# One 8 KB tile for every place of the weight ring, another order ahead of the experts, and small experts in pieces of 2048 and 1536 columns

## The chip, the core and the metric

The kernel runs on one core of one Trainium2 chip, as one program. The time is the device time of one execution in microseconds (us); of several executions the median is given. The engines are named as the profile names them: PE is TensorE, whose weight loads are PEld; DVE is VectorE, ACT is ScalarE, POOL is GpSimd, and SP is SyncE, which here issues almost all transfers.

## The reference

Two residual layers over 256 tokens of 1024 channels, in f32. Each layer has a token mixer (a gated linear recurrence and a differential attention side by side, merged by gates, then an output projection `w_out` of 1024 x 1024) and a channel mixer. In layer 0 the channel mixer is a dense SwiGLU; in layer 1 it is a mixture of eight experts, two of them for each token. All weights are read once, in f32. Cut to what matters here:

```python
def moe_swiglu(h, router, w1, w3, w2):          # w1, w3: 8 x 1024 x 3584, w2: 8 x 3584 x 1024
    logits = t @ router
    vals, idx = lax.top_k(logits, 2)
    comb = sum(one_hot(idx, 8) * softmax(vals)[..., None])
    for e in range(8):
        out += comb[:, e] * ((silu(t @ w1[e]) * (t @ w3[e])) @ w2[e])
```

One expert's w1 and w3 hold 29.36 MB (10^6 bytes) together and its w2 14.68 MB; the eight experts hold 352.3 MB.

## The kernel before

Everything but the experts uses matmuls in which each operand is split in two: `split()` (line 132) has ACT round a weight tile into `wh` (L146) and DVE subtract to get the rest `wl` (L148), and `three()` (L157) issues three matmuls for each tile of weights. `wh` and `wl` are two tiles of 4 KB per partition, four of each. `proj_T()` (line 311) walks over a weight matrix in blocks of 256 columns with eight slabs k of 128 rows; a block is one load of 1 MiB, split in two halves u, and every half gives one group of 128 output columns, which is evacuated when its eight slabs are summed.

The scheduler of the framework orders the instructions of each engine ahead of time, from the order of the program and its own model of durations; on the chip every engine then takes its list in that order, and so does SP with the transfers.

`moe()` (line 759) ends layer 1. While `w_out` is projected, `ev_r` adds each group of the result onto the residual `xT` (L358), squares it (L263) and multiplies it with the router (L799). Then follow, in program order, `rows_rstd()` (matmuls L273, then DVE L257 and POOL L258, which give `r`, the norm of each token), `turn(1)`, which transposes the second half of the residual (PE L753, ACT L786, into `xg`), and `to_bcast()`, which spreads a gate row over the partitions (PE L251, ACT L252, into `g2b`). From `r` a chain of small DVE instructions picks the two experts of each token (L817 to L835, with matmuls L831 to L833), `slots()` builds selection matrices (L858), and `gather()` multiplies them with `xg` (L865) to get the tokens of an expert, X. Only then does the first expert's matmul start.

The experts stand at positions p = 0 to 7. Positions 0, 2, 4 and 6 hold up to 96 tokens ("big"), positions 1, 3, 5 and 7 up to 64 ("small"). An expert is done in four units i: 1024 columns of its 3584 for i = 0 to 2 and 512 for i = 3. `up()` (line 1077) multiplies X with w1 and w3 into the PSUM banks `ups` (L1090, and L1095 for the tokens 64 to 95 of a big expert); ACT and DVE make the gated product from the banks (L1101, L1102, L1107, L1108); PE transposes it (L1117); `down()` (line 1124) multiplies it with w2 into `pds` for a big expert or into `low` for a small one (L1135, L1141), and `finish()` (line 1161) adds the result onto the tokens. The units run in the order up(n), down(n-1), transposes of n, up(n+1), and so on. Experts 0 and 1 are interleaved.

The weights of the experts pass through a ring of 16 places of 1 MiB, each 8 KB in each of 128 partitions. `plan` lists the loads in the order of their use, 42 for each expert, and `ahead()` (line 1045) issues them; a load waits until PE has done with the tile that held the place. Places 0 to 10 are single tiles (six `raw`, five `raw2`, loads at L120). Place 11 is the two halves of `xT`, and places 12 to 15 are four pairs of `wh` and `wl`; these five places are filled by two loads of 512 KB each (L1066), every one of half of the slabs. A load of `up` for i = 0 to 2 takes two slabs of 1024 columns, so every row that it reads in DRAM is 4 KB long; for i = 3 it takes four slabs of 512 columns, rows of 2 KB. A load of w2 reads 8 KB in one run for each partition, or 4 KB in each of two loads where the place is split. The last two loads of the program read w2 in rows of 2 KB.

Of the kernel before, what the change touches and what calls it, by code (L numbers as in the profile page):

```python
# [8 lines left out]
F32 = mybir.dt.float32  # L9
F32R = mybir.dt.float32r  # L10
# [24 lines left out]
CAPS = (96, 64, 96, 64, 96, 64, 96, 64)  # L35
GATHER_AT = {(0, 0): (1, 2), (2, 2): (3, 4), (4, 2): (5, 6), (6, 2): (7,)}
# [12 lines left out]
def hybrid_trunk(ctx: ExitStack, tc: tile.TileContext, x, c, ada_w, ada_b, norm_mix_g, norm_ffn_g, w_in, lb_logits,  # L49
# [113 lines left out]
    const.tile([P, 120], F32, name="gap")  # L163
# [105 lines left out]
    def rows_rstd(acc, ps):  # L269

        for t in range(NT):
            for i, sq in enumerate(acc):
                t_.matmul(ps[:, t:t + 1], lhsT=sq[:, t * P:(t + 1) * P], rhs=ones[:, 0:1], start=i == 0, stop=i == 1)  # L273
        r = small([P, NT], "r", pool=keep)
        rstd(r, ps, D, NT)
        return r
# [34 lines left out]
    def proj_T(w, c0, xh, xl, nk, evac, ncols, order=None):  # L311
# [447 lines left out]
    def moe(y, l, pdp):  # L759
# [15 lines left out]
        small([P, 8], "gap", bufs=1)  # L775
        xs = [small([P, D], "xs") for _ in range(NT)]
# [26 lines left out]
        proj_T(w_out[l], 0, y[0], y[1], KD, ev_r, D)  # L803


        r = rows_rstd(acc, lp[0][:, NE:NE + NT])
# [4 lines left out]
        turn(1)  # L811
        g2b = to_bcast(row, 2, small([P, D], "g2b", bufs=1))
# [125 lines left out]
        def dns(p):  # L938

            return pds if CAPS[p] > 64 else [low]  # L940

# [56 lines left out]
        units = [(0, 0), (0, 1), (1, 0), (0, 2), (1, 1), (0, 3), (1, 2), (1, 3)] + [(p, i) for p in range(2, NE) for i in range(4)]  # L998
        last_ = NE - 1, 3

        def half_of(i):
            return 512 if i < 3 else 256

        def up_srcs(p, i):
            n, c0 = half_of(i), i * 1024
# [5 lines left out]
        def down_srcs(p, i):  # L1011
            n = half_of(i)
            rows_ = n // P

            def view():
                return moe_w2[0, which(p)].rearrange("o (c p k) f -> p (o c) k f", p=P, k=rows_)
            if (p, i) == last_:
                for c in range(2):
                    yield lambda c=c: [view()[:, i * 1024 // n + h, :, c * 512:(c + 1) * 512] for h in range(2)]
                return  # L1020
            for k0 in range(0, rows_, 2):
                for h in range(2):
                    yield lambda c=i * 1024 // n + h, k0=k0: view()[:, c, k0:k0 + 2, :]
# [21 lines left out]
        def ahead(n):  # L1045

            while len(loaded) < min(n, len(plan)):
                src, turn_ = plan[len(loaded)](), len(loaded) % slots_
                k = 4 if isinstance(src, list) else src.shape[1]
                if turn_ >= RAW_BUFS + RAW_MORE:  # L1050
                    if turn_ == RAW_BUFS + RAW_MORE:
                        halves = [xt.rearrange("p k t -> p (k t)") for xt in xT]
                    else:
                        halves = [splp.tile([P, 1024], F32, tag=tag, name=nm("raw")) for tag in ("wh", "wl")]
                else:
                    tag = {"pool": phase[0], "tag": "raw2", "bufs": RAW_MORE} if turn_ >= RAW_BUFS else {"pool": rawp, "tag": "raw"}
                    raw = tag.pop("pool").tile([P, 2048], F32, name=nm("raw"), **tag)
                    halves = [raw[:, h * 1024:(h + 1) * 1024] for h in range(2)]
                    if not isinstance(src, list):
                        load(src, raw, k=k)  # L1060
                        loaded.append(halves)
                        continue
                if not isinstance(src, list):
                    src = [src[:, h * k // 2:(h + 1) * k // 2, :] for h in range(2)]
                for half, part in zip(halves, src):
                    nc.sync.dma_start(half.rearrange("p (k f) -> p k f", k=k // 2), part)  # L1066
# [10 lines left out]
        def up(p, i, xp):  # L1077

            n, rows_, big = half_of(i), half_of(i) // P, CAPS[p] > 64
            nk = 1024 // n  # L1080
            for k0 in range(0, KD, nk):
# [17 lines left out]
            sa = small([P, 512], "sa")  # L1099
            sv = sa[:, :n].rearrange("s (k p) -> s k p", k=rows_)  # L1100
            s_.activation(sv, in_order(ups[0][:, :n]), AF.Silu)  # L1101
            v_.tensor_tensor(sv, sv, in_order(ups[1][:, :n]), op=ALU.mult)  # L1102
            parts = [(sa, 0, P)]
            if big:
                sb = small([P, 512], "sa")
                sv = sb[64:, :n].rearrange("s (k p) -> s k p", k=rows_)
                s_.activation(sv, in_order(ups[2][:64, :n]), AF.Silu)  # L1107
                v_.tensor_tensor(sv, sv, in_order(ups[2][64:, :n]), op=ALU.mult)  # L1108
# [15 lines left out]
        def down(p, i, us):  # L1124
            rows_, dn = half_of(i) // P, dns(p)
            for k0 in range(0, rows_, 2):
                tiles = [next_tile() for _ in range(2)]
                for k in range(k0, k0 + 2):
                    first, last = i == 0 and k == 0, i == (2 if p == NE - 1 else 3) and k == rows_ - 1
# [75 lines left out]
        for n, (p, i) in enumerate(units):  # L1205
            def before_this():
                down(*before)
                if before[:2] in ((before[0], 3), (NE - 1, 2)):
# [51 lines left out]
    for l in range(DEPTH):  # L1260
# [15 lines left out]
        def end_of_mixer(then=None):  # L1276
            acc, ev_x = residual_T(lambda: ada[l, 1]["col"][:, 0:8], then)
            proj_T(w_out[l], 0, y[0], y[1], KD, ev_x, D)
# [81 lines left out]
```

## Time and profile before

| | before |
|---|---|
| median of 3 runs | 1515.84 us (1513.46 to 1518.27) |
| profiled execution, time | 1517.2 us |
| profiled execution, span of its instructions | 1515.4 us |
| mean granted TensorE clock | 0.989 |
| PE busy in the span | 1468.2 us (97%) |
| DVE, ACT busy | 629.6 us (42%), 374.0 us (25%) |
| read from memory | 503.56 MB |

The profiled execution is one execution; its time stands 1.4 us above the median. [...] Busy time of PE counts overlapped matmuls, so 97% does not mean that PE is the limit. Times in the rows are microseconds from the start of the span. The token mixers and the dense layer take the first 660 us, the experts the rest.

### The profile page before, as it was taken

How to read it: one execution, taken by the hardware profiler on the slowest of the kernel's cores; microseconds unless marked ns; L12 is line 12 of the kernel's file. 1: busy time of each engine (PE TensorE's matmuls, PEld its weight loads, DVE VectorE, ACT ScalarE, POOL GpSimd, SP SyncE). 2: the span in 40 equal slices, each digit the busy share in tenths (PEclk: the TensorE clock that was granted, in tenths of full speed). 3: DMA queues.
4: the chain of work that ended last, by engine and by line, in shares of the span. 5: the costliest groups of instructions: out<-in, count | busy, mean ns of one | idle time of the engine just before them, and what ended most of it. 6: DMA issues, size and time to landing. Idle time of an engine off the chain costs nothing.

```text
span 1515.4 us, 29680 instructions
## 1 busy us (share of the span) xinstructions
PE 1468.2 (97%) x12659; PEld 897.3 (59%) x12659; DVE 629.6 (42%) x1046; ACT 374.0 (25%) x618; POOL 33.8 (2%) x34
## 2 busy tenths in 40 slices
PE   5999999999999999999999999999999998999996
PEld 3988999999998899873333333433433433334322
DVE  4898677867788877641100211120021120111202
ACT  3534546544446545320000000000000000000000
POOL 1010100000000100000000000000000000000000
PEclk8999999999999999999999999999999999999999
DMA  9988545668796645858999999999999999999996
GB/s 369 360 300 284 189 142 171 220 225 299 267 339 227 216 146 211 293 213 324 399 418 418 417 421 419 419 420 417 415 420 411 418 420 418 418 415 417 415 423 240
DMA packets 186032, 506.62 MB, mean 334 GB/s; under 512 B 11016, under 2 KB 79252, under 8 KB 170148
## 3 DMA queue, kind: packets, MB, share of 16 engines
q1 hardware_dynamic: 185572, 504.56, 86.0%
q8 instruction: 101, 1.65, 0.4%
q14 instruction: 39, 0.32, 0.1%
q0 software_dynamic: 320, 0.09, 0.0%
HBM read 503.56 MB, written 1.05 MB: 333 GB/s over the span
## 4 chain that ended last, share of the span: by engine, by line
PE 85%; DMA 7%; issue 5%; DVE 1%; SPq 1%; ACT 1%; POOL 0%; DVEq 0%; POOLq 0%; ACTq 0%
PE mm L157 32%; PE mm L1090 24%; PE pd L1135 6%; DMA raw<-in_moe_w_dram 6%; PE at L1095 6%; PE at L1135 4%; PE pd L1141 4%; PE ms L865 2%; PE ms L532 2%; PE ms L1117 1%; DMA raw<-in_ada_w_dram 1%; PE ms L1179 1%; PE ada L229 1%; PE at L615 1%; DVE wl L148 0%
## 5 line engine op out<-in xcount | busy, mean ns | idle before, releaser
L1090 PE MATMUL mm<-raw,X 128*32 128x512 f32 (+1 forms) x3792 | 439.8, 543 | 2.2 <-DMA raw<-in_moe_w_dram 2.1
L1090 PEld LDWEIGHTS mm<-raw,X 128*32 128x32 f32 x3792 | 133.0, 110 | 223.1 <-issue 189.8
L148 DVE TENSOR_TENSOR wl<-raw,wh 128x1024 fp32r<-128x1024 f32 (+1 forms) x188 | 226.8, 1210 | 76.9 <-ACT wh L146 74.4
L146 ACT ACTIVATE wh<-raw 128x1024 fp32r<-128x1024 f32 (+1 forms) x188 | 196.6, 1048 | 177.5 <-PE mm L157 134.5
L1102 DVE TENSOR_TENSOR sa<-sa,mm 128x512 f32<-128x512 f32 (+1 forms) x32 | 19.9, 621 | 464.3 <-PE mm L1090 420.1
L1095 PE MATMUL at<-raw,X 128*32 128x512 f32 (+1 forms) x952 | 171.6, 542 | 0.0
L157 PE MATMUL mm<-hh,wh 128*128 128x256 f32 x576 | 164.2, 285 | 3.6 <-ACT wh L146 3.3
L157 PE MATMUL mm<-hl,wh 128*128 128x256 f32 x576 | 165.0, 287 | 0.0
L157 PE MATMUL mm<-hh,wl 128*128 128x256 f32 x576 | 164.9, 287 | 0.1
L1101 ACT ACTIVATE sa<-mm 128x512 f32<-128x512 f32 (+1 forms) x32 | 17.4, 544 | 516.1 <-PE mm L1090 516.1
L1135 PE MATMUL pd<-raw,u 128*32 128x512 f32 x848 | 121.5, 594 | 0.0
L157 PEld LDWEIGHTS mm<-hh,wh 128*128 128x128 f32 x576 | 110.1, 191 | 5.7 <-ACT wh L146 3.6
L157 PEld LDWEIGHTS mm<-hl,wh 128*128 128x128 f32 x576 | 109.9, 191 | 0.7 <-issue 0.7
L157 PEld LDWEIGHTS mm<-hh,wl 128*128 128x128 f32 x576 | 109.6, 191 | 0.4 <-DVE wl L148 0.4
L1135 PE MATMUL at<-raw,u 128*32 128x512 f32 x816 | 94.0, 594 | 7.0 <-DMA raw<-in_moe_w_dram 6.7
L1141 PE MATMUL pd<-raw,u 128*32 128x512 f32 x424 | 87.4, 592 | 0.0
L1095 PEld LDWEIGHTS at<-raw,X 128*32 128x32 f32 x952 | 46.4, 110 | 60.4 <-issue 54.4
L223 DVE SCALAR_TENSOR_TENSOR raw<-raw,cs,raw 128x2048 f32<-128x2048 f32 x32 | 75.1, 2347 | 8.3 <-DMA raw<-in_ada_w_dram 8.3
L157 PE MATMUL mm<-wh,hh 128*128 128x512 f32 x160 | 64.6, 404 | 0.0
L1135 PEld LDWEIGHTS at<-raw,u 128*32 128x32 f32 x816 | 25.7, 110 | 65.3 <-issue 46.3
L157 PE MATMUL mm<-wl,hh 128*128 128x512 f32 x160 | 64.0, 400 | 0.0
L1135 PEld LDWEIGHTS pd<-raw,u 128*32 128x32 f32 x848 | 31.3, 110 | 54.7 <-issue 51.2
(308 smaller groups left out, 2041.6 us busy)
## 6 DMA issues: line engine op xcount, KB each, us to landing
raw<-in_moe_w_dram SPq DMA_DIRECT2D x231, 1024.0 KB, 14.8
raw<-in_moe_w_dram SPq DMA_DIRECT2D x168, 512.0 KB, 11.1
raw<-in_ada_w_dram SPq DMA_DIRECT2D x47, 1024.0 KB, 4.9
raw<-in_w_in_dram SPq DMA_DIRECT2D x44, 1024.0 KB, 7.4
raw<-in_ffn_w_dram SPq DMA_DIRECT2D x30, 1024.0 KB, 5.1
xT<-in_moe_w_dram SPq DMA_DIRECT2D x42, 512.0 KB, 16.5
raw<-in_w_out_dram SPq DMA_DIRECT2D x8, 1024.0 KB, 4.7
raw<-in_w_branch_a_dram SPq DMA_DIRECT2D x4, 1024.0 KB, 5.1
```

The costliest lines, as they stand in the source:

```text
L146: s_.activation(wh[:, c], r[:, c], AF.Copy)
L148: v_.tensor_tensor(wl[:, c], r[:, c], wh[:, c].bitcast(F32), op=ALU.subtract)
L157: t_.matmul(ps, lhsT=lhs, rhs=rhs, start=first and i == 0, stop=last and i == 2)
L223: v_.scalar_tensor_tensor(got["acc"], raw, cs[:, k:k + 1], got["acc"], op0=ALU.mult, op1=ALU.add)
L532: t_.matmul(ps[:, at_:at_ + HD].rearrange("p (g w) -> p g w", w=H), lhsT=kq[:, h, i * P:(i + 1) * P], rhs=rhs, start=True, stop=True)
L865: t_.matmul(ps[:, i * n:(i + 1) * n], lhsT=xg[t][:, k * P:(k + 1) * P], rhs=pm[:, t, :n], start=t == 0, stop=t == NT - 1)
L1090: t_.matmul(ups[m][q:q + 32, :n], lhsT=xp[:, k, 32 * s:32 * s + 32], rhs=rhs[m][h], start=k == 0, stop=k == KD - 1)
L1095: t_.matmul(ups[2][q:q + 32, :n], lhsT=xp[:, k, 64:96], rhs=rhs[m][h], start=k == 0, stop=k == KD - 1)
L1101: s_.activation(sv, in_order(ups[0][:, :n]), AF.Silu)
L1102: v_.tensor_tensor(sv, sv, in_order(ups[1][:, :n]), op=ALU.mult)
L1135: t_.matmul(dn[0][q:q + 32, :], lhsT=us[0][:, k, 64 * h + 32 * s:64 * h + 32 * s + 32], rhs=rhs[h][c], start=first and h == 0, stop=last a ...
L1141: t_.matmul(dn[1][q:q + 32, :], lhsT=us[1][:, k, 32 * h:32 * h + 32], rhs=rhs[h][c], start=first, stop=last)
```

## The change

Four edits are made together.

1. `wh` and `wl` become the two halves of one tile of 8 KB, and the two halves of `xT` become one tile. All 16 places of the ring are then single tiles, each filled by one load of 1 MiB (only the last two loads of the program still come as pairs). The small tiles that pad the layout are moved, not resized in sum.
2. The small experts at positions 3, 5 and 7 are cut into other pieces: 2048 and 1536 columns for 3 and 5, and 2048, 1024 and 512 for 7. A load of `up` in such a wide piece takes one slab of the full width, rows of 8, 6 or 4 KB (tiles of 1 MiB, 768 KB and 512 KB). `up` uses four banks for a wide piece: `ups[0:2]`, and `ups[2]` with `low` for the second 1024 columns; the last 512 of a 1536 share one bank. The results of `down` go to `pds[0]` in place of `low`. The last piece of 512 columns keeps the old form.
3. `proj_T` gets an argument `late`, which both `w_out` projections set to 2: for the first block, both halves are split first, then slabs 0 to 5 of both groups are multiplied, and then slabs 6 and 7 of both.
4. In `moe`, `turn(1)` and `to_bcast` are held on PE behind the last matmul of `rows_rstd`.

```diff
+NARROW, WIDE = (1024, 1024, 1024, 512), (3, 5, 7)
+WIDTHS = (NARROW, NARROW, NARROW, (2048, 1536), NARROW, (2048, 1536), NARROW, (2048, 1024, 512))
...
-        wh = splp.tile([P, 1024], F32R, tag="wh", name=nm("wh"))[:, :n]
-        wl = splp.tile([P, 1024], F32R, tag="wl", name=nm("wl"))[:, :n]
+        both = splp.tile([P, 2048], F32R, tag="w", name=nm("w"))
+        wh, wl = both[:, :n], both[:, 1024:1024 + n]
...
-    xT = [const.tile([P, 4, S], F32, name=f"xT{h}") for h in range(2)]
+    const.tile([P, 96], F32, name="gap0")
+    xT_all = const.tile([P, KD, S], F32, name="xT")
+    xT = [xT_all[:, 4 * h:4 * h + 4, :] for h in range(2)]
...
+                if late and b0 == 0:
+
+                    parts = [split(raw[:, :, u * P:(u + 1) * P]) for u in range(2)]
+                    ps = [mm() for _ in range(2)]
+                    for ks in (range(kn - late), range(kn - late, kn)):
+                        for gg, (wh, wl) in enumerate(parts):
+                            for k in ks:
+                                three(ps[gg][:, :n_], xh[k // 4][:, k % 4, :], xl[k // 4][:, k % 4, :], wh[:, k, :], wl[:, k, :],
+                                      k == 0, k == nk - 1, True)
+                            if kn - 1 in ks:
+                                evac(gg, ps[gg][:, :n_])
+                    continue
...
-        proj_T(w_out[l], 0, y[0], y[1], KD, ev_r, D)
+        proj_T(w_out[l], 0, y[0], y[1], KD, ev_r, D, late=2)
...
-        r = rows_rstd(acc, lp[0][:, NE:NE + NT])
+        r = rows_rstd(acc, lp[0][:, NE:NE + NT], behind)
...
-        turn(1)
-        g2b = to_bcast(row, 2, small([P, D], "g2b", bufs=1))
+        with tc.issue_after(behind[0]):
+            turn(1)
+            g2b = to_bcast(row, 2, small([P, D], "g2b", bufs=1))
...
-            return pds if CAPS[p] > 64 else [low]
+            return pds if CAPS[p] > 64 else [pds[0] if p in WIDE else low]
...
+            if is_wide(p, i):
+                for k in range(KD):
+                    for wm in (moe_w1, moe_w3):
+                        yield lambda wm=wm, k=k: wm[0, which(p)].rearrange("o (k p) f -> p (o k) f", p=P)[:, k:k + 1, c0:c0 + WIDTHS[p][i]]
+                return
...
-                if turn_ >= RAW_BUFS + RAW_MORE:
-                    if turn_ == RAW_BUFS + RAW_MORE:
-                        halves = [xt.rearrange("p k t -> p (k t)") for xt in xT]
-                    else:
-                        halves = [splp.tile([P, 1024], F32, tag=tag, name=nm("raw")) for tag in ("wh", "wl")]
+                if turn_ > RAW_BUFS + RAW_MORE:
+                    raw = splp.tile([P, 2048], F32, tag="w", name=nm("raw"))
+                elif turn_ == RAW_BUFS + RAW_MORE:
+                    raw = xT_all.rearrange("p k t -> p (k t)")
...
+            if is_wide(p, i):
+                full = [ups[:2], [ups[2], low]][:width // 1024]
+                shared = ups[2] if width % 1024 else None
+                for k in range(KD):
+                    tiles = [next_tile() for _ in range(2)]
+                    for j, banks in enumerate(full):
+                        for m in range(2):
+                            for h in range(2):
+                                for s in range(2):
+                                    q = 32 * (2 * h + s)
+                                    t_.matmul(banks[m][q:q + 32, :], lhsT=xp[:, k, 32 * s:32 * s + 32],
+                                              rhs=tiles[m][j][:, h * 512:(h + 1) * 512], start=k == 0, stop=k == KD - 1)
```

## Rows read from the trace of the kernel before

**Rows 1.** The page's part 2: data rate in 40 slices of 37.9 us.
```profile
GB/s 369 360 300 284 189 142 171 220 225 299 267 339 227 216 146 211 293 213 324 399 418 418 417 421 419 419 420 417 415 420 411 418 420 418 418 415 417 415 423 240
```

**Rows 2.** Windows of the experts' stage: length, busy times, granted clock, DMA share, GB/s.
```profile
740.00:1490.00 750.00, 736.82 (x7078) 264.99 (x7074) 98.51 (x187) 46.32 (x84) 0.00 (x0) 1.00 1.02 418
1440.00:1460.00 20.00, 19.12 (x178) 5.99 (x174) 1.44 (x3) 1.31 (x3) 0.00 (x0) 1.00 1.02 418
1462.00:1480.00 18.00, 15.64 (x144) 4.33 (x132) 0.69 (x1) 1.19 (x2) 0.00 (x0) 1.00 1.01 426
1482.00:1492.00 10.00, 8.69 (x112) 3.20 (x102) 2.19 (x3) 0.63 (x1) 0.00 (x0) 1.00 1.04 405
1495.00:1500.00 5.00, 3.85 (x46) 1.63 (x48) 1.26 (x3) 0.77 (x2) 0.00 (x0) 1.00 0.46 174
905.00:910.00 5.00, 5.00 (x48) 1.65 (x44) 0.87 (x2) 0.60 (x1) 0.00 (x0) 1.00 1.00 419
1405.00:1420.00 15.00, 15.00 (x140) 4.59 (x136) 0.29 (x1) 0.38 (x1) 0.00 (x0) 1.00 1.02 404
1270.00:1275.00 5.00, 3.29 (x63) 1.50 (x54) 0.00 (x0) 0.39 (x1) 0.00 (x0) 1.00 1.04 425
```

**Rows 3.** The chain that ended last: start, length, what, in stretches of the experts' stage.
```profile
788.84 13.87 PE mm L1090 x128
...
1072.44 15.63 DMA raw<-in_moe_w_dram
```

**Rows 4.** Windows ahead of the first expert and at its start.
```profile
635.00:640.00 5.00, 5.00 (x25) 5.00 (x25) 2.70 (x3) 1.68 (x4) 0.00 (x0) 0.50 1.03 418
...
665.00:670.00 5.00, 4.17 (x19) 4.13 (x20) 4.25 (x26) 1.33 (x2) 0.00 (x0) 0.54 0.13 53
670.00:675.00 5.00, 5.00 (x37) 3.77 (x40) 4.22 (x20) 0.00 (x0) 0.00 (x0) 0.78 0.01 3
...
700.00:705.00 5.00, 5.00 (x43) 3.26 (x35) 0.92 (x4) 0.00 (x0) 0.00 (x0) 1.00 0.29 118
```

**Rows 5.** SP's transfers in order of time: start, length of the stretch, line, count.
```profile
662.42 0.33 SPq L1066 DMA_DIRECT2D xT<-in_moe_w_dram  x1
678.70 34.08 SPq L120 DMA_DIRECT2D raw<-in_moe_w_dram  x11
```

**Rows 6.** The page's part 6: loads of 1 MiB, count, KB, median landing.
```profile
raw<-in_moe_w_dram SPq DMA_DIRECT2D x231, 1024.0 KB, 14.8
```

**Rows 7.** PE in order of time, from the last projection to the first experts.
```profile
658.57 1.02 PE L251 MATMUL at<-sa,ident 128*128 128x512 f32 x2
...
662.54 0.36 PE L273 MATMUL ms<-ones,sqk 128*128 128x1 f32 x2
665.54 0.58 PE L831 MATMUL at<-mask,upper 128*128 128x16 f32 x2 [2.64 <-DVE wt L844]
...
667.26 6.13 PE L865 MATMUL ms<-pm,xg 128*128 128x96 f32 x32 [0.28 <-DVE pm L858]
...
702.14 3.53 PE L865 MATMUL ms<-pm,xg 128*128 128x160 f32 x24
```

**Rows 8.** ACT and DVE in order of time, at the end of the projection.
```profile
659.35 0.42 ACT L263 ACTIVATE sqk<-xT 128x256 f32<-128x256 f32 x1 [2.46 <-DVE xT L358]
...
662.95 0.16 DVE L257 TENSOR_SCALAR r<-ms 128x2 f32<-128x2 f32 x1 [3.69 <-PE ms L273]
```

**Rows 9.** PE and DVE in order of time, at the start of that projection.
```profile
624.90 0.28 PE L157 MATMUL mm<-yh,wh 128*128 128x256 f32 x1
...
629.52 0.28 PE L157 MATMUL mm<-yh,wl 128*128 128x256 f32 x1
632.87 0.39 PE L157 MATMUL mm<-yl,wh 128*128 128x256 f32 x1 [3.07 <-DVE yl L674]
...
631.79 0.69 DVE L773 TENSOR_TENSOR sa<-sa,row 128x512 f32<-128x512 f32 x1 [3.54 <-DMA sa<-in_ada_b_dram]
```

**Rows 10.** The page's part 5: matmuls of `three`.
```profile
L157 PE MATMUL mm<-hh,wh 128*128 128x256 f32 x576 | 164.2, 285 | 3.6 <-ACT wh L146 3.3
```

More of the change, by code (lines that the diff above doesn't have):

```diff
@@ L309, in norm_T, with proj_T @@
         return hs, ls
-    def proj_T(w, c0, xh, xl, nk, evac, ncols, order=None):
+    def proj_T(w, c0, xh, xl, nk, evac, ncols, order=None, late=0):
         cw, n_ = 512 if nk == 4 else 256, xh[0].shape[2]
@@ L1048, in ahead @@
                 src, turn_ = plan[len(loaded)](), len(loaded) % slots_
-                k = 4 if isinstance(src, list) else src.shape[1]
-                if turn_ >= RAW_BUFS + RAW_MORE:
-                    if turn_ == RAW_BUFS + RAW_MORE:
-                        halves = [xt.rearrange("p k t -> p (k t)") for xt in xT]
-                    else:
-                        halves = [splp.tile([P, 1024], F32, tag=tag, name=nm("raw")) for tag in ("wh", "wl")]
-                else:
[L1056 to L1066, printed above, removed]
+                if turn_ > RAW_BUFS + RAW_MORE:
+                    raw = splp.tile([P, 2048], F32, tag="w", name=nm("raw"))
+                elif turn_ == RAW_BUFS + RAW_MORE:
+                    raw = xT_all.rearrange("p k t -> p (k t)")
+                elif turn_ >= RAW_BUFS:
+                    raw = phase[0].tile([P, 2048], F32, tag="raw2", bufs=RAW_MORE, name=nm("raw"))
+                else:
+                    raw = rawp.tile([P, 2048], F32, tag="raw", name=nm("raw"))
+                halves = [raw[:, h * 1024:(h + 1) * 1024] for h in range(2)]
+                if isinstance(src, list):
+                    for half, part in zip(halves, src):
+                        nc.sync.dma_start(half.rearrange("p (k f) -> p k f", k=2), part)
+                else:
+                    load(src, raw, k=src.shape[1])
                 loaded.append(halves)
@@ L1077, in up @@
         def up(p, i, xp):
-            n, rows_, big = half_of(i), half_of(i) // P, CAPS[p] > 64
+            n, rows_, big = half_of(p, i), half_of(p, i) // P, CAPS[p] > 64
             nk = 1024 // n
-            for k0 in range(0, KD, nk):
+            width = WIDTHS[p][i]
+            full, shared = [ups[:2]], ups[2] if big else None
+            if is_wide(p, i):
[10 more added lines that the diff above has]
+                                              rhs=tiles[m][j][:, h * 512:(h + 1) * 512], start=k == 0, stop=k == KD - 1)
+                    if shared is not None:
+                        for m in range(2):
+                            for s in range(2):
+                                q = 32 * (2 * m + s)
+                                t_.matmul(shared[q:q + 32, :], lhsT=xp[:, k, 32 * s:32 * s + 32], rhs=tiles[m][1][:, :512],
+                                          start=k == 0, stop=k == KD - 1)
+            for k0 in range(0, 0 if is_wide(p, i) else KD, nk):
                 tiles = [next_tile() for _ in range(2)]
@@ L1124, in down @@
         def down(p, i, us):
-            rows_, dn = half_of(i) // P, dns(p)
+            rows_, dn = half_of(p, i) // P, dns(p)
+            end_ = len(WIDTHS[p]) - (2 if p == NE - 1 else 1)
+            if is_wide(p, i):
+                n_chunks = WIDTHS[p][i] // 512
+                chunks = [us[c // 2][:, :, 64 * (c % 2):64 * (c % 2) + 64] for c in range(n_chunks)]
+                for q0 in range(0, n_chunks, 2):
+                    for k0 in range(0, rows_, 2):
+                        for ch in range(q0, min(q0 + 2, n_chunks)):
+                            tile_ = next_tile()
+                            for k in range(k0, k0 + 2):
+                                first, last = i == 0 and ch + k == 0, i == end_ and ch == n_chunks - 1 and k == rows_ - 1
+                                for c in range(2):
+                                    for s in range(2):
+                                        q = 32 * (2 * c + s)
+                                        t_.matmul(dn[0][q:q + 32, :], lhsT=chunks[ch][:, k, 32 * s:32 * s + 32],
+                                                  rhs=tile_[k - k0][:, c * 512:(c + 1) * 512], start=first, stop=last)
+                return
             for k0 in range(0, rows_, 2):
@@ L1128, in down @@
                 for k in range(k0, k0 + 2):
-                    first, last = i == 0 and k == 0, i == (2 if p == NE - 1 else 3) and k == rows_ - 1
+                    first, last = i == 0 and k == 0, i == end_ and k == rows_ - 1
                     rhs = [[tiles[h][k - k0][:, c * 512:(c + 1) * 512] for c in range(2)] for h in range(2)]
```

57 lines of the change are left out of this document (34 added, 23 removed).

## The prediction

> **What bounds the kernel now.** I read the slices of the page first, because the four edits lie in different stages. From slice 20 on, the data rate stands between 411 and 424 GB/s until the last slice [rows 1], and over 740 to 1490 us it is 418 GB/s at a DMA share of 1.02 [rows 2]: the transfers are busy without a gap, although PE also reads as busy (736.8 of 750 us). Which of the two sets the end is read from the chain: until shortly before 1072 us it runs through PE, then it crosses to landings of weights, 15.63 us in one piece at 1072 [rows 3]. A unit of 1024 columns for a small expert takes PE 13.87 us for 8 tiles [rows 3], 1.73 us a tile, while a tile of 1.049 MB at 418 GB/s takes 2.51 us. So in the experts' stage time is bytes over rate, and PE has slack.
>
> Ahead of that stage PE decides. The 16 tiles that fit into the ring have landed by about 667 us, and the data rate falls to 53 and 3 GB/s [rows 4], because the next load waits at SP until 678.70 for PE to free the first place [rows 5]. A first expert that starts x earlier moves this and all later loads x earlier: there x counts in full.
>
> **Part 1, the transfers.** Prices by length of row in DRAM come from the tail, where the plan tells which loads are in flight. The last six tiles (6.3 MB) are read in rows of 2 KB, the eight before them (8.4 MB) in rows of 8 KB, all in whole places. Landing ends at about 1497 (174 GB/s in the window of 1495 to 1500 means 2.1 us of work), so 1482 to 1492 is 2 KB, 405 GB/s, and 1462 to 1480 is 8 KB, 426 GB/s [rows 2]. The price of 4 KB is what is left of the long window: 750 us x 418 = 313.5 MB; 1/7 of two thirds of it is 2 KB (29.9 MB, 73.7 us), 11/16 of the w2 third is 8 KB (71.8 MB, 168.6 us), and the other 211.8 MB take 507.7 us, 417 GB/s. That is 2.469, 2.397 and 2.347 us per MB for 2, 4 and 8 KB; for 6 KB, a third of the way from 8 to 4 in 1/length, 2.364.
>
> What changes its row: w2 in the five split places, 5/16 of 117.4 MB = 36.7 MB, from 4 to 8 KB; the three pieces of 2048 columns, 50.3 MB, from 4 to 8; the last 1536 of experts 3 and 5, 16.8 MB from 4 to 6 and 8.4 MB from 2 to 6. So 87.0 x 0.050 + 16.8 x 0.033 + 8.4 x 0.105 = 4.35 + 0.55 + 0.88 = 5.8 us less. Lower bound: one window of 8 KB rows shows 419 GB/s [rows 2], no better than 4 KB; then only the 0.88 remains.
>
> The 105 tiles in split places (5/16 of 336) now come as 210 loads of 512 KB; they become 105 loads. The split places fill at 404 GB/s in one stretch (1405 to 1420) and at 418 in another (1440 to 1460) [rows 2]. With all 18 rounds of 5.24 MB at 404 instead of 417 the gain would be 94 MB x 0.078 = 7.4 us, otherwise nothing; I take 1.2, near the lower end, since the mean of 417 already holds the slow stretches. Transfers together: 7.0 us less, bounds 0.9 and 13.2.
>
> [...]
>
> **Part 2, the wide units on PE.** Each matmul of 512 columns reappears with another bank; the last 512 columns need half as many matmuls, twice as wide. PE's 1.73 us a tile stays, and is hidden by the 2.51 us of the transfer. A wide piece of 2048 has four banks to read out before the next `up`: two passes of DVE, each about the 0.69 us of its pass over 128x512 [rows 9], behind the first of ACT, some 2.3 us, but the `down` of the unit before lies between (at least 2 tiles, 3.5 us of PE), so nothing is charged; uncovered, five wide pieces would cost 11.5 us. `pds[0]` is read by `finish` a whole unit before the next expert's first `down`. Tiles of 768 and 512 KB let the ring hold less in time, but a load of 1 MiB lands 14.8 us after its issue [rows 6], six times its own 2.51, so the queue stays fed. Zero.
>
> **Part 3, one tile for `wh` and `wl`, and for `xT`.** A place is now free when both halves are. The last reader is a `wh` matmul in any case, so PE waits as now: 3.6 us before 576 matmuls [rows 10]. Zero; at most one matmul of 0.285 us per wait. The first half of `xT` can no longer be loaded early: the 1 MiB goes out when `turn(1)` has read the tile, about 662.4 us as its second half does now [rows 5]. If SP has it ahead of the four loads of the places behind, these wait with it, 12.6 us of transfers, which still end before 678.70. PE needs that tile 11 tiles after its start. Zero; 2.5 us if a transfer had been waiting.
>
> **Part 4, `late`.** In layer 1 PE stands 3.07 us before a `yl` matmul, because the `yl` instructions stand on DVE behind L773, which waits 3.54 us for a small transfer [rows 9]. `late` puts 36 matmuls ahead of the last two slabs. But from 624.90 to 629.52 [rows 9], 40 starts 0.12 us apart, the list had already run 40 of the block's 48 before it stopped: the scheduler mixes the two groups already, and the new order has two fewer ahead, 0.2 us more. What DVE waits for is not touched. In layer 0 PE runs through without a gap; the second split is needed one group earlier, at most one DVE pass of 1.2 us. I take +0.2, bounds 0 and +1.4.
>
> **Part 5, the order ahead of the experts.** The last square is ready at 659.77 and the norm `r` starts on DVE at 662.95 [rows 8]. Between them PE does the two broadcasts (1.02 us each pair of records) and the transposes, and the matmuls L273 end only at 662.90 [rows 7]. The eight records of L273 cost 4 x 0.36 = 1.4 us, so without the others `r` starts at 661.2, 1.75 us earlier. The moved work is at most 662.90 - 658.57 - 1.4 = 2.9 us. It runs from 661.2 to 664.1, and L831, now ready at 665.54 - 1.75 = 663.8, is queued behind it and loses 0.3. The copies into `xg` finish before `gather` needs them. Net 1.4 us less, bounds 0 (a broadcast in front of L831 as long as the gain) and 1.75.
>
> The same move fills a hole. [...] With the moved work inside the hole I expect the clock to hold: 1.7 us less; if it falls all the same, 0.
>
> **Sum.** -7.0 + 0.2 - 1.4 - 1.7 = -9.9 us. The profiled execution took 1517.2, which gives 1507.3; it stood 1.4 above the median of 1515.84, so the median forecast is 1505.9.
>
> **The rivals.**
> *Longer rows bring little.* The rate is set by something other than the row, as the 419 at 905 to 910 would have it. Then the transfers save 0.9 and the rest 2.9: 1512. If the 426 of the end is half due to the row and half to what else the tail lacks, the rows save 2.9 in place of 5.8: 1508.8. Against both: 426 over 18 us. [...]
> *The stop before `yl` goes too.* If the new list of DVE has L773 behind the `yl` instructions, 3.07 us of waiting go, and half of at least 5 us at clock 0.50 that follow [rows 4, 9]: 5.6 more, 1500.3. Nothing in the change moves L773; only another list would.
> [...]
>
> **How the numbers follow.** Forecast, with its front and row terms within 4 us: 0.55. Little from the rows (half or none): 0.22. The `yl` stop gone: 0.12. Clock or another stop in the wide units: 0.11, of which 0.09 lie beyond the bound. About 0.3% (4.5 us, the spread of the three runs) is what can be told from no change, so faster means under 1511.3. The forecast and the `yl` case lie there, and a third of the row rival: 0.74. The rest of it, and a little of the clock case, is the same: 0.17. Slower: 0.09. The range 1499 to 1513 runs from the `yl` case to the rival without any gain from rows, and leaves 2 in 10 out.
>
> **What would show it.** Right: windows over experts 3, 5 and 7 at 421 to 426 GB/s and none near 404; L273 ahead of L251, and `r` 1.5 us after the last square, now 3.2; a clock of 1.00 during the first `gather`. Wrong: a data rate of 418 in wide pieces of 8 KB rows; SP issuing the first load into a used place of the ring still 18.9 us after the last square (now 659.77 to 678.70), where I expect 15.8; DMA share below 1.0 within the experts' stage; a clock under 1.00 in units 3, 5 or 7.

## The result and the profile after

The kernel after takes 1505.88 us (median of 6 runs, 1503.97 to 1508.63), the kernel before 1515.9 (6 runs beside them, 1513.46 to 1518.27): ratio 0.994, 95% interval 0.9925 to 0.9955. The forecast was 1505.9. The profiled execution of after took 1504.83 us with a span of 1502.9; before had 1517.2 and 1515.4.

The page's part 2 (data rate in 40 slices, here of 37.6 us) and part 6 (loads) of the kernel after answer to [rows 1, 6]:
```profile
GB/s 370 363 296 293 176 155 175 211 238 287 269 340 244 198 168 197 269 248 332 395 420 420 418 423 420 420 414 425 421 421 420 426 424 422 423 422 417 420 420 263
...
raw<-in_moe_w_dram SPq DMA_DIRECT2D x283, 1024.0 KB, 17.7
...
raw<-in_moe_w_dram SPq DMA_DIRECT2D x30, 768.0 KB, 13.9
xT<-in_moe_w_dram SPq DMA_DIRECT2D x19, 1024.0 KB, 18.3
raw<-in_moe_w_dram SPq DMA_DIRECT2D x19, 512.0 KB, 10.9
```
The slices of the experts' stage now read mostly 420 to 426, where they read mostly 415 to 420. Whole places of 1 MiB are 283 and 19 loads, the split places are gone, and a load lands 17.7 us after its issue instead of 14.8. An estimate from rate and landing time has about 7.5 MB on the way at once (421 GB/s x 17.7 us), before 6.2 (418 x 14.8), so the queue is no worse fed.

Windows of the experts' stage, kernel after (columns as in [rows 2]; the clock is the granted share of full speed):
```profile
740.00:1455.00 715.00, 711.19 (x6682) 249.13 (x6677) 99.39 (x187) 43.74 (x78) 0.00 (x0) 1.00 1.02 421
...
950.00:1060.00 110.00, 109.22 (x1042) 39.65 (x1038) 19.11 (x42) 7.17 (x13) 0.00 (x0) 1.00 1.01 420
1150.00:1270.00 120.00, 119.22 (x1136) 42.92 (x1132) 19.21 (x40) 7.77 (x14) 0.00 (x0) 1.00 1.02 424
1360.00:1455.00 95.00, 94.12 (x920) 35.07 (x916) 15.20 (x26) 6.58 (x12) 0.00 (x0) 1.00 1.02 419
...
985.00:990.00 5.00, 5.00 (x48) 1.60 (x44) 0.29 (x1) 0.38 (x1) 0.00 (x0) 1.00 0.96 390
1405.00:1420.00 15.00, 15.00 (x148) 4.53 (x144) 0.00 (x0) 0.00 (x0) 0.00 (x0) 1.00 1.01 425
1425.00:1430.00 5.00, 5.00 (x52) 1.66 (x48) 1.38 (x2) 1.10 (x2) 0.00 (x0) 1.00 1.02 388
...
1470.00:1480.00 10.00, 8.24 (x84) 2.40 (x76) 2.19 (x3) 0.63 (x1) 0.00 (x0) 1.00 1.04 407
```
The same long window of the kernel before reads:
```profile
740.00:1455.00 715.00, 705.63 (x6774) 255.35 (x6770) 96.32 (x184) 44.68 (x81) 0.00 (x0) 1.00 1.02 418
```
The window of 1405 to 1420, which stood at 404 [rows 2], stands at 425. But a window at a fixed time holds other loads in each kernel, and low ones are left: 390 at 985 to 990 with a DMA share of 0.96, 388 at 1425 to 1430, and 407 in the tail with its rows of 2 KB. The stretches around the wide pieces of experts 3, 5 and 7 (950 to 1060, 1150 to 1270, 1360 to 1455) read 420, 424 and 419; in the run without wide pieces below they read 417, 420 and 419. The predicted sign of 421 to 426 shows in one of the three. PE's idle time in the long window falls from 9.4 to 3.8 us: its slack is nearly used up. The chain of the kernel after shows the same thing from the other side (columns as in [rows 3]):
```profile
797.27 1.72 PE pd L1204 x16
799.85 1.72 PE pd L1204 x16
...
1053.17 12.15 PE pd L1192 x112
...
1263.90 17.83 DMA raw<-in_moe_w_dram
```
It crosses to the landings of weights in long pieces at 1264 us, before at 1072 [rows 3]. Until then it runs through PE: a w2 tile of a big expert takes PE 2.58 us (797.27 to 799.85), a little more than the 2.49 us of its transfer at 421 GB/s.

Ahead of the experts, kernel after: engines in order of time (columns as in [rows 5, 7, 8, 9]).
```profile
623.13 0.40 PE L159 MATMUL mm<-yh,w 128*128 128x256 f32 x2
...
631.55 0.58 PE L159 MATMUL mm<-yl,w 128*128 128x256 f32 x1 [3.52 <-DVE yl L691]
...
630.47 0.69 DVE L790 TENSOR_TENSOR sa<-sa,row 128x512 f32<-128x512 f32 x1 [3.99 <-DMA sa<-in_ada_b_dram]
...
658.71 0.42 ACT L267 ACTIVATE sqk<-xT 128x256 f32<-128x256 f32 x1 [2.43 <-DVE xT L375]
...
660.21 0.16 DVE L261 TENSOR_SCALAR r<-ms 128x2 f32<-128x2 f32 x1 [1.59 <-PE ms L277]
...
659.81 0.36 PE L277 MATMUL ms<-ones,sqk 128*128 128x1 f32 x2
660.04 1.07 PE L770 MATMUL mm<-ident,xT 128*128 128x128 f32 x8
660.94 1.88 PE L255 MATMUL at<-sa,ident 128*128 128x512 f32 x4
662.81 0.37 PE L850 MATMUL at<-mask,upper 128*128 128x16 f32 x2
...
664.12 3.81 PE L884 MATMUL ms<-pm,xg 128*128 128x96 f32 x32 [0.50 <-DVE pm L877]
667.87 1.92 PE L1141 MATMUL mm<-raw,X 128*32 128x512 f32 x16
...
674.12 5.09 SPq L122 DMA_DIRECT2D raw<-in_moe_w_dram  x4
```
Read it against [rows 7, 8]: the matmuls of the norm come first, `r` starts 1.08 us after the last square (660.21 against 658.71 + 0.42) where it was 3.18, the transposes and broadcasts run where PE was idle for 2.64 us, and the 32 matmuls of the gather take 3.81 us where they took 6.13. Against [rows 9]: the stop ahead of `yl` is still there, 3.52 us instead of 3.07, and the low clock behind it too (columns as in [rows 4]):
```profile
635.00:640.00 5.00, 5.00 (x25) 5.00 (x25) 2.29 (x3) 1.12 (x3) 0.00 (x0) 0.50 1.03 417
...
665.00:670.00 5.00, 5.00 (x47) 3.45 (x49) 4.71 (x24) 0.00 (x0) 0.00 (x0) 1.00 0.17 64
```

**Three stages.** Three landmarks of each trace divide the time: the first `yh` matmul of the last `w_out`, the end of the last square, and the first matmul of an expert. Before: 624.90, 659.77, 673.32, end 1515.4 [rows 7 to 9]. After: 623.13, 659.13, 667.87, end 1502.9. So of -12.5 us in the profiled pair, -1.8 lies ahead of `w_out`, +1.1 from there to the last square, -4.8 from there to the first expert and -7.05 in the experts. The experiments below are read by the same three lengths, since medians of different kernels lie only a few us apart.

### The profile page after: what moved, and what is told of

It reads as the page before. It is cut to its first block, busy times and chain, and to the rows that moved or that the text cites. A ratio compares the mean times of both kernels' runs of the same rounds, so it can differ in the third digit from the quotient of the medians.

```text
span 1502.9 us, 29132 instructions
## 1 busy us (share of the span) xinstructions
PE 1467.1 (98%) x12535; PEld 884.9 (59%) x12535; DVE 632.8 (42%) x1051; ACT 372.1 (25%) x613; POOL 33.8 (2%) x34
## 4 chain that ended last, share of the span: by engine, by line
PE 89%; DMA 7%; DVE 1%; SPq 1%; ACT 1%; issue 0%; POOL 0%; ACTq 0%; DVEq 0%; POOLq 0%
PE mm L159 35%; PE mm L1141 16%; PE pd L1204 7%; PE at L1146 6%; DMA raw<-in_moe_w_dram 5%; PE mm L1124 5%; PE pd L1210 4%; PE at L1124 3%; PE pd L1192 2%; PE ms L549 2%; PE at L1204 2%; PE ms L884 1%; DMA raw<-in_ada_w_dram 1%; PE ms L1170 1%; PE at L1130 1%; PE ms L1248 1%
## 5 line engine op out<-in xcount | busy, mean ns | idle before, releaser
L1141 PE MATMUL mm<-raw,X 128*32 128x512 f32 (+1 forms) x2496 | 308.4, 536 | 1.7 <-DMA raw<-in_moe_w_dram 1.7
L150 DVE TENSOR_TENSOR w<-raw,w 128x1024 fp32r<-128x1024 f32 (+1 forms) x188 | 226.8, 1210 | 75.0 <-ACT w L148 72.7
L148 ACT ACTIVATE w<-raw 128x1024 fp32r<-128x1024 f32 (+1 forms) x188 | 196.6, 1048 | 175.7 <-PE mm L159 133.2
L159 PE MATMUL mm<-hh,w 128*128 128x256 f32 x1152 | 213.0, 286 | 3.5 <-ACT w L148 3.1
L159 PEld LDWEIGHTS mm<-hh,w 128*128 128x128 f32 x1152 | 180.7, 191 | 6.1 <-ACT w L148 3.5
L159 PE MATMUL mm<-hl,w 128*128 128x256 f32 x576 | 164.9, 286 | 0.0
L1154 ACT ACTIVATE sa<-mm 128x512 f32<-128x512 f32 (+1 forms) x27 | 14.8, 550 | 512.3 <-PE mm L1141 407.7
L1204 PE MATMUL pd<-raw,u 128*32 128x512 f32 x848 | 122.0, 594 | 0.0
L159 PEld LDWEIGHTS mm<-hl,w 128*128 128x128 f32 x576 | 109.7, 190 | 0.7 <-issue 0.7
L159 PE MATMUL mm<-w,hh 128*128 128x512 f32 x320 | 104.9, 402 | 0.0
L1124 PE MATMUL mm<-raw,X 128*32 128x512 f32 x720 | 99.2, 595 | 0.0
L1210 PE MATMUL pd<-raw,u 128*32 128x512 f32 x424 | 87.7, 592 | 0.0
L1192 PE MATMUL pd<-raw,u 128*32 128x512 f32 x608 | 67.5, 593 | 1.4 <-DMA raw<-in_moe_w_dram 1.4
## 6 DMA issues: line engine op xcount, KB each, us to landing
raw<-in_moe_w_dram SPq DMA_DIRECT2D x283, 1024.0 KB, 17.7
```

What stands on the lines that cost most here:

```text
L159: t_.matmul(ps, lhsT=lhs, rhs=rhs, start=first and i == 0, stop=last and i == 2)
L1124: t_.matmul(banks[m][q:q + 32, :], lhsT=xp[:, k, 32 * s:32 * s + 32], rhs=tiles[m][j][:, h * 512:(h + 1) * 512], start=k == 0, stop=k == K ...
L1141: t_.matmul(ups[m][q:q + 32, :n], lhsT=xp[:, k, 32 * s:32 * s + 32], rhs=rhs[m][h], start=k == 0, stop=k == KD - 1)
L1192: t_.matmul(dn[0][q:q + 32, :], lhsT=chunks[ch][:, k, 32 * s:32 * s + 32], rhs=tile_[k - k0][:, c * 512:(c + 1) * 512], start=first, stop= ...
L1204: t_.matmul(dn[0][q:q + 32, :], lhsT=us[0][:, k, 64 * h + 32 * s:64 * h + 32 * s + 32], rhs=rhs[h][c], start=first and h == 0, stop=last a ...
L1210: t_.matmul(dn[1][q:q + 32, :], lhsT=us[1][:, k, 32 * h:32 * h + 32], rhs=rhs[h][c], start=first, stop=last)
```

## The experiments

Their own 17 runs of the kernel before have medians of 1516.3 (first four kernels) and 1516.0 us (the next four).

**The order alone**, on the kernel before:
```diff
+        behind = []
-        r = rows_rstd(acc, lp[0][:, NE:NE + NT])
+        r = rows_rstd(acc, lp[0][:, NE:NE + NT], behind)
...
-        turn(1)
-        g2b = to_bcast(row, 2, small([P, D], "g2b", bufs=1))
+        with tc.issue_after(behind[0]):
+            turn(1)
+            g2b = to_bcast(row, 2, small([P, D], "g2b", bufs=1))
```


> The kernel before with the fourth edit alone (turn(1) and to_bcast held on PE behind rows_rstd). If the order pays what the two traces show at the first expert (L865 began 3.1 us earlier against the last square, and the gather ran at full clock, 6.13 to 3.81 us), the first expert starts 4 to 5 us earlier after the last square and the time falls by 3 to 5 us, to about 1512, with the transfers at 417 to 418 GB/s as before. If instead the whole gain of the change comes from the transfers and the earlier start is swallowed by the ring, the time stays at 1515.9 within 1.5 us.

Measured: 1511.36 us (1508.59 to 1514.49, 12 runs), ratio 0.997 (0.9961 to 0.998). From the last square to the first expert it is 8.74 us, as in the kernel after. The gather begins 5.0 us after the last square where it was 7.5; the 3.1 us of the expectation compare times from the start of the span. The experts take 843.4, 1.0 to 1.3 us more than in the two executions of before (842.1, 842.4); why is open.

**All but the order**, on the kernel after:
```diff
-        with tc.issue_after(behind[0]):
+        if True:
```


> The changed kernel without its fourth edit. If the edits add up, it loses the same 3 to 5 us: 1509 to 1511, with r again some 3 us after the last square and the granted clock again near 0.5 during the first gather. If the order gave nothing, 1505.9 within 1.5 us.

Measured: 1509.42 us (1508.16 to 1510.83, 6 runs), ratio 0.9959 (0.9945 to 0.9973). PE of this kernel in order of time:
```profile
664.16 0.58 PE L850 MATMUL at<-mask,upper 128*128 128x16 f32 x2 [2.64 <-DVE wt L863]
...
665.88 5.95 PE L884 MATMUL ms<-pm,xg 128*128 128x96 f32 x32 [0.29 <-DVE pm L877]
671.75 1.92 PE L1141 MATMUL mm<-raw,X 128*32 128x512 f32 x16
```
The hole of 2.64 us and the slow gather are back as they were before, at 0.50 of the clock in 665 to 670 us, and the first expert comes 13.37 us after the last square. The order, and nothing else of the change, fills the hole.

**No wide pieces**, on the kernel after:
```diff
-NARROW, WIDE = (1024, 1024, 1024, 512), (3, 5, 7)
-WIDTHS = (NARROW, NARROW, NARROW, (2048, 1536), NARROW, (2048, 1536), NARROW, (2048, 1024, 512))
+NARROW, WIDE = (1024, 1024, 1024, 512), ()
+WIDTHS = (NARROW,) * 8
```


> The changed kernel with all eight experts in pieces of 1024, 1024, 1024 and 512, so rows of 4 and 2 KB for w1 and w3 everywhere; single ring tiles, late and the new order stay. By the prices of the prediction the wide pieces are worth 50.3 x 0.050 + 16.8 x 0.033 + 8.4 x 0.105 = 3.9 us: 1509.8. If the length of the row does not set the rate, 1505.9 within 1.5 us. If wide pieces hurt PE, less than 1505.

Measured: 1508.47 us (1508.01 to 1512.28, 6 runs), ratio 0.9958 (0.9942 to 0.9973). The experts take 838.9 us here and 835.0 in the kernel after, where the forecast had 3.95 us for the wide pieces. Between the medians lie 2.6, with overlapping intervals.

**Without `late`**, on the kernel after:
```diff
-        proj_T(w_out[l], 0, y[0], y[1], KD, ev_r, D, late=2)
+        proj_T(w_out[l], 0, y[0], y[1], KD, ev_r, D)
```
(and the same at layer 0.)


> The changed kernel with the old loop in both w_out projections. The prediction gave late +0.2 us, bounds 0 and +1.4, so 1505.7, no difference that can be told. The rival: late is why the last projection started 1.8 us earlier in the profile after; then the time rises by 1 to 2 us, to 1507 to 1508.

Measured: 1503.87 us (1503.04 to 1507.21, 6 runs), ratio 0.9928 (0.9912 to 0.9943). PE of this kernel, then its windows:
```profile
630.63 0.39 PE L159 MATMUL mm<-yl,w 128*128 128x256 f32 x1 [2.67 <-DVE yl L691]
```
```profile
630.00:635.00 5.00, 3.86 (x21) 3.69 (x22) 3.88 (x7) 2.62 (x4) 0.00 (x0) 0.74 1.03 422
635.00:640.00 5.00, 5.00 (x28) 5.00 (x28) 1.08 (x3) 0.49 (x1) 0.00 (x0) 0.58 1.02 415
```
The first `yh` matmul starts at 623.06, no later than with `late`, so `late` is not what brought `w_out` forward; the stop is 2.67 us instead of 3.52. `late` costs time if anything, but 2.0 us between overlapping intervals is not a measured size.

**The ring alone**: the kernel before with single 8 KB places (one tile for `wh` and `wl`, one for `xT`), narrow pieces, no `late`, no new order; the diff is the kernel after without its other three edits.


> Edit 1 alone on the kernel before: one 8 KB place instead of two 4 KB halves, no wide pieces, no new order, no late planes. Theory of the sum: 36.7 MB less price 0.050 us each plus 1.2 us for half as many transfers give -3.0 us, and -1.8 us more if the one tile for wh and wl is why the variants that have it reach w_out at about 623 us instead of 625: 1511 to 1512 us, with the first yh matmul of w_out at 623. Rival: only the transfers count, 1513.3 us with w_out at 625. Rival: half as many transfers of the same bytes bring nothing, 1516 us. If the earlier start is due to the clock, PE shows granted clock 1.00 in 205 to 215 us, where the kernel before shows 0.80 and 0.86.

Measured: 1513.3 us (1511.47 to 1514.96, 12 runs), ratio 0.9984 (0.9974 to 0.9994). The experts take 838.5 us (before 842.1 and, in a second execution, 842.4): the ring is worth 3.8 there, against the forecast's 36.7 x 0.050 + 1.2 = 3.0. The first `yh` matmul stands at 623.29 and the clock in 205 to 215 us at 1.00, as the theory of an earlier start had it, but the median shows only -2.7 us; the repeated runs below say why.

**Rows by themselves.** A kernel that leaves out all arithmetic streams expert weights into a ring, stage after stage.
```diff
+    def rows4(e, j):
+        return [up(e, 2 * (j % 4), 2, 1024 * (j // 4 % 3), 1024)]
+    def rows4_halved(e, j):
+        return [up(e, 2 * (j % 4) + h, 1, 1024 * (j // 4 % 3), 1024) for h in range(2)]
+    def rows8(e, j):
+        return [up(e, j % 8, 1, 0, 2048)]
...
+    kinds = (rows4, rows8, rows4_halved, rows6, w2_whole, rows2, w2_halved)
```


> The kernel leaves all arithmetic out: it only streams expert weights into a 16-place ring, 24 places per stage, in seven stages, twice over: w1 rows of 4 KB, of 8 KB, of 4 KB in half-size loads, of 6 KB, w2 rows of 8 KB whole (two rows a partition), w1 rows of 2 KB, w2 in half-size loads (one row of 4 KB a partition). Theory (the price is the row length): the data rate by stage orders itself 2 KB, 4 KB, 6 KB, 8 KB, about 405, 417, 422 and 426 GB/s, and the half-size loads lie within 1 GB/s of the whole ones at the same row length. Rival (the number of loads sets the price): the half-size stages fall to about 405 GB/s, and 4 KB and 8 KB rows in whole loads are the same. Rival (the ring's refill sets it, not the queue): all stages equal within 1 GB/s.

Measured, one execution. Windows inside the stages of the first turn, in the order of `kinds` (length, POOL's busy time, clock, DMA share, GB/s):
```profile
20.00:60.00 40.00, 0.00 (x0) 1.00 1.03 410
80.00:120.00 40.00, 0.00 (x0) 1.00 1.01 422
140.00:180.00 40.00, 0.00 (x0) 1.00 1.03 409
195.00:225.00 30.00, 0.00 (x0) 1.00 1.02 418
240.00:280.00 40.00, 0.00 (x0) 1.00 1.01 422
300.00:340.00 40.00, 0.00 (x0) 1.00 1.05 387
365.00:405.00 40.00, 0.00 (x0) 1.00 1.03 409
```
The second turn differs by 1 GB/s at most. Rows of 2, 4, 6 and 8 KB give 387, 410, 418 and 422 GB/s, w1 and w2 alike, and half-size loads cost nothing (409 against 410): in this bare stream the length of the contiguous row sets the price, the number of loads does not. The step from 2 to 8 KB is 35 GB/s, where the expectation had 21 (405 to 426).

A second stream loads w1 and w3 in turns, and mixes them with w2:
```diff
+    def both(e, j, nk, c0, n):
+        return [(up, up3)[j % 2](e, nk * (j // 2 % (8 // nk)), nk, c0, n)]
+    def both4(e, j):
+        return both(e, j, 2, 1024 * (j // 8 % 3), 1024)
...
+    kinds = (both4, both8, rows4, both6, mixed4, both2, mixed8)
```


> Streaming alone once more, all arithmetic left out, 24 places a stage, but with w1 and w3 in turn as the experts load them: rows of 4 KB, of 8 KB, of 4 KB from w1 alone, of 6 KB, then two places of w1 and w3 in 4 KB rows beside one of w2 in 8 KB, rows of 2 KB, and the same mixture with 8 KB rows. In the stream of w1 alone 4 KB rows gave 410 GB/s and 8 KB rows 422, while the whole kernel before, two thirds of whose bytes are in 4 KB rows, ran at 418. Theory (a stream from one tensor is slower than a stream in turns): 4 KB in turns about 417, 8 KB about 424 to 426, the mixtures 418 and 424. Rival (the row alone sets the price, and the rate in the kernel is read too high): 410 and 422 again, the mixtures 414 and 422.

Windows inside the first, second, fifth and seventh stage (columns as in the stream before):
```profile
20.00:60.00 40.00, 0.00 (x0) 1.00 1.03 410
80.00:120.00 40.00, 0.00 (x0) 1.00 1.01 422
...
240.00:280.00 40.00, 0.00 (x0) 1.00 1.02 414
...
365.00:405.00 40.00, 0.00 (x0) 1.00 1.01 422
```
The theory fell: taking tensors in turns changes nothing. The mixture with 4 KB rows streams at 414 GB/s, while the kernel before reaches 418 with a similar one. What makes the kernel's stream faster than a bare one stays open.

**The row addition later**, on the kernel after. L790, the addition that waits on DVE for the small load of `ada_b` ahead of `yl`, is held behind the fifth residual addition of that projection:
```diff
-        v_.tensor_tensor(row, row, ada[l, 2]["row"], op=ALU.add)
...
-        acc, ev_x = residual_T(lambda: ada[l, 1]["col"][:, 0:8])
+        adds = []
+        acc, ev_x = residual_T(lambda: ada[l, 1]["col"][:, 0:8], None, adds)
...
+        with tc.issue_after(adds[4]):
+            v_.tensor_tensor(row, row, ada[l, 2]["row"], op=ALU.add)
```


> The kernel after, with the addition of ada_b's row to the router's row held on VectorE until the fifth residual addition of layer 1's w_out, so that VectorE does not wait for that load ahead of the split of yl. Theory (PE sets the end of this stage, the wait for yl is on its path and the clock's fall follows the wait): the stall of 3.5 us ahead of yl goes, granted clock stays 1.00 through 630 to 645 us, the first refill leaves 5 to 8 us earlier than 674.1 us: 1498 to 1501 us. Rival (the ring was full and PE's loss is given back later): the gather comes earlier and the time stays 1505.9 us. Rival (only the stall, not the clock): -3.5 us, 1502.4 us.

Measured: 1499.24 us (1497.14 to 1501.68, 6 runs), ratio to before 0.9894 (0.9876 to 0.9911). Windows of this kernel:
```profile
630.00:635.00 5.00, 4.49 (x38) 4.32 (x38) 3.69 (x6) 2.70 (x5) 0.00 (x0) 1.00 1.02 384
635.00:640.00 5.00, 5.00 (x45) 5.00 (x44) 3.53 (x5) 2.66 (x4) 0.00 (x0) 1.00 1.03 419
640.00:645.00 5.00, 5.00 (x46) 5.00 (x44) 1.89 (x5) 1.51 (x3) 0.00 (x0) 1.00 1.02 419
```
The stop is gone, and the clock holds 1.00 where it read 0.55, 0.50 and 0.92. From the first `yh` matmul to the last square it is 28.4 us instead of 36.0, and the median comes down by 6.6, so nearly all of it reaches the end. The rivals fell: it is more than the stop's 3.5, and it is not given back.

**The row addition later and no `late`**, which is the run before with the edit of the fourth.


> The kernel of the run before this one with late=0 as well, so that w_out has the old order of its k planes. Without late the run of the kernel after gained 2.0 us. Theory (late only reorders, and costs its own PE time): 2 us off again, 1496 to 1499 us. Rival (late pays once the row addition is out of the way, since the planes of yl are what is late then): 1 to 2 us slower than with late.

Measured: 1500.13 us (1496.38 to 1501.45, 6 runs), ratio 0.9901 (0.9885 to 0.9918). Neither theory held. `w_out` to the last square takes 28.4 us with and without `late`; without the stop, `late` has no effect that can be told.

**Three kernels once more, unchanged.**


> The kernel before once more, unchanged, for a second profiled execution. The question is the fall of granted clock behind the gap of 1.9 us near 206 us: it is there in the kernel before, in the order-only kernel and in the one with the later row addition, and not in six others with the same PE work. Theory (it hangs on the program): 0.80 and 0.86 in 205 to 215 us again. Rival (it comes or stays away by execution): one of the three repeated kernels shows the other value, about 1.7 us earlier or later at w_out.

> The kernel after once more, unchanged. Theory (it hangs on the program): granted clock 1.00 in 205 to 215 us and 0.55, 0.50, 0.92 in 630 to 645 us again, w_out at 623.1 us. Rival (by execution): one of these differs, by 1.5 us or more of PE time.

> The kernel with the later row addition once more, unchanged. Theory (it hangs on the program): 0.77 and 0.89 in 205 to 215 us and 0.68 in 655 to 660 us again. Rival (by execution): 1.00 in 205 to 215 us, or the fall ahead of the gather missing.

One execution each, 1514.4, 1507.58 and 1498.29 us. Windows around 210 us, kernel before again:
```profile
205.00:210.00 5.00, 3.11 (x25) 2.82 (x25) 3.65 (x5) 2.32 (x3) 0.70 (x1) 1.00 0.25 52
210.00:215.00 5.00, 5.00 (x45) 5.00 (x44) 3.47 (x8) 2.88 (x5) 0.00 (x0) 1.00 0.46 161
```
and kernel after again:
```profile
205.00:210.00 5.00, 3.09 (x18) 2.80 (x18) 3.66 (x5) 2.33 (x3) 0.73 (x1) 0.82 0.19 51
210.00:215.00 5.00, 5.00 (x39) 5.00 (x38) 2.03 (x6) 1.52 (x3) 0.00 (x0) 0.84 0.46 163
```
Each shows what the other kernel showed in its first profile (0.80 and 0.86 before, 1.00 and 1.00 after). So the fall behind this gap (PE idle for 1.45 us until DVE's `od`, then for 0.45 us until ACT's `oh`) comes or stays away by execution, and the 1.8 us ahead of `w_out` in the first pair is no effect of the change: in the second pair it is +1.4 (623.54 and 624.91). The third kernel showed 0.77 and 0.89, then 0.78 and 0.88, but its fall ahead of the gather (0.68 in 655 to 660) was missing the second time. Its two executions ran on different chips, so chip and execution aren't told apart there.

The three lengths of all profiled executions, from the landmarks defined above (us, worked out; `yh` to square, square to expert, expert to the end of the span):
```
before, before again        34.87 34.10   13.55 12.42   842.1 842.4
order alone                 33.26          8.74         843.4
ring alone                  35.60         13.56         838.5
after without wide pieces   35.16         10.20         838.9
after without the order     35.12         13.37         835.3
after without late          34.43          8.73         835.4
after, after again          36.00 35.38    8.74 10.21   835.0 835.3
row addition later, again   28.42 28.47   10.21  8.73   835.0 834.8
  and without late          28.39          8.74         834.8
```
The third length takes three values: 842 to 843 without the new ring, 838 to 839 with it, 835 with the wide pieces as well; order, `late` and the later addition do not move it to another. The second takes two with the new order, 8.7 and 10.2. In the slower one the broadcasts L255 take 3.4 to 3.5 us instead of 1.88, with a granted clock of 0.68 to 0.78 in the window that holds most of them (kernel after again: 0.72 in 660 to 665), and L850 (L831 of the kernel before) stands behind them. The kernel after again:
```profile
662.10 3.52 PE L255 MATMUL at<-sa,ident 128*128 128x512 f32 x4
665.41 0.40 PE L850 MATMUL at<-mask,upper 128*128 128x16 f32 x2
```

## Why the prediction was right

The sum was -9.9 and the medians show -10.0. The mechanisms hold and the terms have the right sign. The agreement to a tenth is luck: `late` cost 0.8 us more than forecast, the order and the clock brought 0.8 more, and inside the transfers other errors cancel as well. By its steps:

- **What bounds.** Right. The experts' stage follows the data rate, and a first expert that starts earlier ends earlier: order alone is -4.9 us in the median, where its second length is 8.74 against a mean of 13.0 in the two executions of before; and with the row addition later the first length is some 7 us shorter while the third stays at 834.8 to 835.0. But that PE has slack was read from a small expert's tile alone (1.73 us). A big expert's takes 2.58, more than its transfer. The slack was that of the whole stage, 9.4 us of 715 before and 3.8 after; whether a gain much above 7 us would still reach the end was not tried.
- **Transfers, -7.0 (0.9 to 13.2).** The third length falls by 7.1 in both pairs. Its halves came out near their prices: ring 3.8 (3.0 forecast), wide pieces 3.3 to 3.7 against the mean of after, 835.2 (0.050 x 50.3 + 0.55 + 0.88 = 3.95). What lies inside is less sure. At the stream's rates the rows were priced too low: 87.0, 16.8 and 8.4 MB are worth 6.0 + 0.8 + 1.6 = 8.4 us in place of 5.8, and half as many loads are worth nothing in place of 1.2. These two errors go against each other. But by the same rates the ring's 36.7 MB are worth 2.5 us, and it gave 3.8, while the wide pieces are worth 5.9 and gave 3.3 to 3.7. So the stream's prices do not carry over to the kernel part by part, and whether the 1.3 us that the ring gave beyond its rows come from the halved number of loads is not shown. The upper bound counts 18 rounds of split places where 105 tiles are 21; it would be 14.4.
- **Wide units on PE, one tile for `wh` and `wl`: 0.** Right as far as shown: over the long window the clock reads 1.00 and the DMA share 1.02, and PE's wait for ACT's `w` stays small (3.5 us before the 1152 matmuls that now carry both halves, [rows 10] 3.6). One predicted sign of an error, a DMA share below 1.0, did show for some 10 us (0.98 in 980 to 985 and 0.96 in 985 to 990). That the wide units cost nothing is not shown either: the wide pieces fell 0.3 to 0.7 us short of 3.95, and no run says by what.
- **`late`, +0.2 (0 to +1.4).** Direction right, size probably too low. Four executions with it have 35.1 to 36.0 in the first length, five without have 33.3 to 35.6; the means differ by 1.0. The step that was off is the reason: the list had run the same 40 matmuls before it stopped in both orders, so it is not two matmuls fewer. What differs is the small load of `ada_b`: DVE's addition starts 7.1 to 7.4 us after the issue of that load in the four with `late` (kernel after: 623.37 to 630.47), 6.3 to 6.7 in the five without, and PE's stop is 3.5 to 3.8 us against 2.7 to 3.1. Why it lands later was not tried. The 1.0 is a mean over kernels that differ in other edits too, and the two ranges overlap.
- **Order, -1.4, and clock, -1.7.** The 1.7 of the clock is a term of the sum that no run shows by itself. What the traces show in its place: behind the hole of 2.64 us, at clocks of 0.54 and 0.78, the gather takes 6.13 us [rows 4, 7]; with the moved work in the hole it takes 3.81 in all eight executions, where an estimate for its 32 matmuls from the 24 of 160 columns in 3.53 us [rows 7] is 4.7. Right in direction, a little low in size: the mean of the second length falls from 13.2 (four executions without it) to 9.3 (eight with it), 3.9 us against 3.1. `r` came 1.08 us after the square and not 1.5, since the four pairs of L277 start 0.22 us apart and overlap, where the prediction added up their full 0.36. L831's queueing was priced at 0.3; it is 0 in five executions and 1.4 to 1.5 in the three of 10.2, where the gather took its 3.81 us all the same and the moved broadcasts 3.4 to 3.5 instead of 1.88. The first refill left 15.0 us after the last square in the first execution and 16.5 in the second, around the 15.8 of the forecast.
- **The sum** of the measured terms is -7.1 + 1.0 - 3.9 = -10.0; with the spread of the lengths, that it meets the medians exactly is chance. The profiled pair's own -12.5 holds -1.8 of clock ahead of `w_out` and the better of the two outcomes in the gather: one profile of each would have given the order 0.9 too much.
- **The rivals.** Rows and ring together brought what was priced; how much of it is the rows is open, as said above. The stop ahead of `yl` stayed, as argued, since no edit moves L773. Its price was 5.6 us (3.07 and half of 5); taken away by an edit of its own it gave 6.6 in the median, because the low clock lasted over parts of three windows (0.55, 0.50 and 0.92 from 630 to 645 us in the kernel after). In a wide unit no fall of the clock shows: 1.00 over 950 to 1060, 1150 to 1270 and 1360 to 1455 us.

## What to carry to other kernels

When transfers bound a stage, count the contiguous bytes of each row before counting the loads: from 4 KB to 8 KB the bare stream gained 3% of its rate (410 to 422 GB/s), and from half as many loads nothing (409 against 410). Then measure in the kernel, where the parts came out otherwise than in the stream. Where PE bounds a stage, look for the instruction on another engine that waits for a small transfer ahead of what PE needs: moving one addition behind it gave two thirds of what four edits gave, since the low clock behind the wait cost about as much as the wait (6.6 us in all, of which the wait is 3.52). And divide two traces by landmarks before believing their difference; the lengths between them repeated within 1.5 us, that of the experts within 0.4, where spans moved by 3.

## What was not expected of the hardware

Behind the same gap of PE (1.45 and 0.45 us near 206 us) the granted clock stayed at 1.00 in one execution of a program and read 0.82 and 0.84 over the next two windows in another, (0.18 + 0.16) x 5 = 1.7 us of PE's work; behind the hole of 2.6 us ahead of L831 it read 0.50 to 0.67 in 665 to 670 us in all four executions that have the hole. With the hole filled it still fell in three of eight, over the broadcasts ahead of the gather (0.68 to 0.78). A bare stream of weights was slower than the whole kernel with a similar mixture of rows (414 against 418 GB/s); why is open.
